# Overflow rounds of a routed mixture of experts: one loop on the chip in place of four unrolled copies

## The chip, the cores and the metric

The kernel runs on one core of a Trainium2 chip. The metric is the device time of one execution in microseconds (us), the median over several runs. Five engines work side by side, each with its own stream of instructions: TensorE (PE for matmuls, PEld for its weight loads), VectorE (DVE), ScalarE (ACT), GpSimd (POOL) and SyncE (SP), which here issues nearly all transfers. They are kept in step by semaphores.

## The reference

Two decoder layers over 512 tokens of width 1024, in float32. A layer has a combined input projection, three kinds of attention, an output projection with a layer norm, and then a mixture of 16 experts of which each token uses two:

```python
gates = jnp.sum(jax.nn.one_hot(expert_idx, N_EXPERTS, dtype=jnp.float32) * w[..., None], axis=1)
h = jax.nn.silu(jnp.einsum('nd,edf->enf', xt, w_gate)) * jnp.einsum('nd,edf->enf', xt, w_up)
h = h * gates.T.astype(h.dtype)[:, :, None]
y = jnp.einsum('enf,efd->nd', h, w_down)
```

Each expert has two 1024 x 256 matrices (gate and up) and one 256 x 1024 matrix (down). How many tokens an expert gets depends on the data.

## The kernel before

A small planner (the class `Flow`) runs while the program is built: every piece of work is a stream of steps with an assumed engine and cost, and the planner writes the instructions of all streams into one fixed order for each engine. Nothing of that order is decided on the chip.

The experts are computed sparsely. Each expert has `CAP` = 96 slots, so the 16 experts fill 1536 rows, which are `NP` = 12 passes of 128 rows. For a pass, GpSimd gathers 128 token rows (`gather`, line 1293), TensorE transposes them (line 1503), multiplies with gate and up (`s_passes`, line 1594), ScalarE and VectorE form silu(gate) times up (lines 1472 and 1473), TensorE transposes that (line 1500) and multiplies with down (`second`, line 1568), and GpSimd scatters the rows to a scratch tensor in HBM (`scatter`, line 1298). SP streams the expert weights ahead of use (lines 1355, 1357 and 1361, `s_load_experts`), as buffers come free. On TensorE the work of one pass stands in the order: transposes of line 1500 and 1503, the down product of the pass before it (line 1568, 32 matmul records), the gate and up product of the next (line 1594, 64 records).

An expert that gets more than 96 tokens is finished by `overflow` (lines 1369 to 1417). It first reads on every engine the largest count of tokens of any expert into a register (line 1370) and branches on it:

```python
many = nc.values_load(mosti[0:1, 0:1], min_val=0, max_val=S)
...
with tc.If(many > CAP):
```

Inside stand ceil((512 - 96) / 128) = 4 rounds. Each round marks which token sits in which of the next 128 overflow slots of every expert (`slot_hot`, line 1385), builds a table of rows by matmuls (`table_mm`), and then runs a loop on the chip over the 16 experts that gathers, multiplies and scatters 128 rows each. The rounds were written out four times by a Python loop; only the loop over experts is a loop on the chip (`tc.For_i`). When no expert has more than 96 tokens, every engine jumps over all of this. Behind the jump stands a short piece that waits for the semaphores that the skipped part would have moved and moves them on; SP's and GpSimd's part of it waits for transfers.

The planner places `overflow` as one step of 0.5 us on TensorE, in the midst of the passes. In the built order it falls, in both layers, between the two halves of a down product of line 1568, ahead of the gate and up product of pass 10 (counted from 0). The planner does not see how many instructions the step holds.

Of the kernel before, what the change touches and what calls it, by code (L numbers as in the profile page):

```python
# [11 lines left out]
OP = mybir.AluOpType  # L12
# [4 lines left out]
P = 128  # L17
D = 1024
S = 512
NT = S // P  # L20
# [4 lines left out]
CAP = 96  # L25
# [170 lines left out]
def body(tc, sb, pp, dr, x, w_in, attn_sinks, c_q_norm_g, c_kv_norm_g, w_uq, w_ukv, w_out, ln1_g, ln1_b,  # L196
         w_router, router_bias, w_gate, w_up, w_down, ln2_g, ln2_b, rope, out):
    nc = tc.nc
    V, A, G, T, SY = nc.vector, nc.scalar, nc.gpsimd, nc.tensor, nc.sync
# [25 lines left out]
    def fixed(*shape):  # L225
        n = 1
        for d in shape:
            n *= d
        return view(take_f(n), *shape)
# [18 lines left out]
    smalls = {}  # L248
# [45 lines left out]
    iotf = fixed(P)  # L294
# [49 lines left out]
    slot_hot = [sb.tile([P, P], BF16, name=f"sl{i}") for i in range(8)]  # L344
    slot_val = [sb.tile([P, 16 * NE], BF16, name=f"rv{i}") for i in range(2)]

    def val(q, w):
        return slot_val[q][:, :16 * w].rearrange("p (k m i e) -> p k m i e", k=4, m=2, i=2)
# [59 lines left out]
    def rshape(w, *shape):  # L408
        n = 1
        for d in shape:  # L410
            n *= d
        v = w[:, :n]
        if len(shape) == 2:
            v = v.rearrange("p (a b) -> p a b", b=shape[1])
        if len(shape) == 3:
            v = v.rearrange("p (a b c) -> p a b c", b=shape[1], c=shape[2])
        return v
# [61 lines left out]
    def layer(l, xready, prev_free):  # L479
# [738 lines left out]
        def table_mm(pt, w):  # L1218
            for j in range(8):
                for m in range(2):  # L1220
                    T.matmul(pt[:, :2 * w], slot_hot[j], val(j // 4, w)[:, j % 4, m].rearrange("p a b -> p (a b)"), start=j + m == 0,
                             stop=j == 7 and m == 1)

        def table_set(pt, ti, w):
            V.tensor_scalar(ti[:, :, :w], pt[:, :2 * w].rearrange("p (a b) -> p a b", b=w), FAR, None, op0=OP.add)
# [66 lines left out]
        def gather(g, idx):  # L1292
            G.indirect_dma_start(out=g, out_offset=None, in_=XD[l][:, :],
                                 in_offset=bass.IndirectOffsetOnAxis(ap=idx, axis=0),
                                 bounds_check=S - 1, oob_is_err=False)

        def scatter(yo, idx):
            return G.indirect_dma_start(out=YD[l][:, :], out_offset=bass.IndirectOffsetOnAxis(ap=idx, axis=0),
                                        in_=yo, in_offset=None, bounds_check=2 * S - 1, oob_is_err=False)
# [69 lines left out]
        def overflow():  # L1369
            many = nc.values_load(mosti[0:1, 0:1], min_val=0, max_val=S)  # L1370
            ps, acc = [g[1] for g in ov["PS"]], [g[1] for g in ov["ACC"]]
            r0, w8, r2 = ov["RAW"][0][1], ov["RAW"][1][1].rearrange("p (a b) -> p a b", b=512), ov["RAW"][2][1]
            w2 = ov["RAW"][1][1].rearrange("p (a b) -> p a b", b=D)
            g, yo, gt = r0[:, :D], r0[:, D:], rshape(r2, KD, P)
            si, hx, ht = r2[:, D:D + FE], r2[:, D + FE:D + 2 * FE], rshape(r2[:, D + 2 * FE:], 2, P)
            with tc.If(many > CAP):  # L1376
                for q in range(NT // 2):

                    V.tensor_tensor(smalls["row", q], smalls["posk", q], smalls["eb", q], op=OP.subtract)
                    oh4 = smalls["oh", q].rearrange("p (k o e) -> p k o e", k=4, o=1).to_broadcast([P, 4, 2, NE])  # L1380
                    V.tensor_scalar(val(q, NE)[:, :, 0], oh4, pcol, None, op0=OP.mult)
                    V.tensor_tensor(val(q, NE)[:, :, 1], oh4, rowc[q].to_broadcast([P, 4, 2, NE]), op=OP.mult)
                for r in range(-(-(S - CAP) // P)):
                    for j in range(8):
                        V.tensor_scalar(slot_hot[j], iotf, float(r * P), smalls["row", j // 4][:, j % 4:j % 4 + 1],
                                        op0=OP.add, op1=OP.is_equal)
                    table_mm(ps[0], NE)
                    table_set(ps[0], tidx[1], NE)
                    with tc.For_i(0, NE, 1) as e:
                        V.tensor_copy(idx2[:, 0:1], tidx[1][:, 0, bass.ds(e, 1)])  # L1390
                        V.tensor_copy(idx2[:, 1:2], tidx[1][:, 1, bass.ds(e, 1)])
                        G.memset(g, 0.0)
                        gather(g, idx2[:, 0:1])
                        for b in range(2):
                            pb = ps[b].rearrange("p (a b) -> p a b", b=P)
                            for j in range(4):
                                T.transpose(pb[:, j], g[:, (4 * b + j) * P:(4 * b + j + 1) * P], ident)
                            A.copy(gt[:, 4 * b:4 * b + 4], pb)
                        for u in range(2):
                            us = slice(u * 512, (u + 1) * 512)  # L1400
                            SY.dma_start(w8[:, :, :FE], w_gate[l, bass.ds(e, 1), us, :].rearrange("o (k p) c -> p (o k) c", p=P))
                            SY.dma_start(w8[:, :, FE:], w_up[l, bass.ds(e, 1), us, :].rearrange("o (k p) c -> p (o k) c", p=P))
                            for j in range(4):
                                k = 4 * u + j
                                T.matmul(acc[0], gt[:, k], w8[:, j], start=k == 0, stop=k == KD - 1)
                        A.activation(si, acc[0][:, :FE], AF.Silu)
                        V.tensor_tensor(hx, si, acc[0][:, FE:], op=OP.mult)
                        pb = ps[0].rearrange("p (a b) -> p a b", b=P)
                        for j in range(2):
                            T.transpose(pb[:, j], hx[:, j * P:(j + 1) * P], ident)  # L1410
                        A.copy(ht, pb[:, :2])
                        SY.dma_start(w2, w_down[l, bass.ds(e, 1)].rearrange("o (k p) c -> p (o k) c", p=P))
                        for n in range(2):
                            for j in range(2):
                                T.matmul(acc[1], ht[:, j], w2[:, j, n * 512:(n + 1) * 512], start=j == 0, stop=j == 1)
                            A.copy(yo[:, n * 512:(n + 1) * 512], acc[1])
                        scatter(yo, idx2[:, 1:2])
# [4 lines left out]
        def s_overflow():  # L1422
            yield E("most")
            yield E("near")
            yield E("gu", NP - 3)
            ov["RAW"] = yield Take(RAW2, 3)
            ov["PS"], ov["ACC"] = [], []
            for _ in range(2):
                ov["PS"].append((yield Take(PS)))
            for _ in range(2):  # L1430
                ov["ACC"].append((yield Take(ACC)))
            e = yield pe(0.5, overflow, [max(flow.free.values())])
            for k in ("A", "V", "G", "D", "GD"):
                flow.free[k] = max(flow.free.get(k, 0.0), e)
            for g in ov["RAW"]:
                put_raw(g, e)
            for g in ov["PS"]:
                PS.put(g, e)
            for g in ov["ACC"]:
                ACC.put(g, e)  # L1440
            flow.set(E("over"), e)
# [335 lines left out]
```

## Time and profile before

| what | value |
|---|---|
| runs: median of 3 (lowest to highest) | 863.41 us (861.07 to 863.6) |
| profiled execution, its own time | 862.1 us |
| its span, first to last instruction | 860.3 us |
| TensorE busy | 821.7 us, 96% of the span |
| mean granted TensorE clock | 0.988 of full |
| expert stage of layer 0 / of layer 1 | about 240 to 412 us / 680 to 828 us of the span |

The profile is of one execution. Busy times are sums over an engine's instructions; TensorE's matmuls are pipelined, so a busy TensorE is not one at its peak. The name PEq (or PEldq, DVEq, ACTq, SPq, POOLq) stands for an engine's sequencer, which does branches, register loads and semaphores; these don't count as busy. q8 and q14 are the queues over which instructions themselves are fetched.

### The profile page before, as it was taken

What the parts mean: (1) busy time and instruction counts of PE and PEld (TensorE: products, weight loads), DVE (VectorE), ACT (ScalarE), POOL (GpSimd) and SP (SyncE); (2) the same over time, 40 slices, a digit from 0 to 9 for tenths busy, and PEclk for the clock granted to TensorE, in tenths of its full rate; (3) what the DMA queues carried; (4) which work ended last, traced back from release to release, by engine and by line L of the source; (5) the groups of instructions that cost most, each with busy time, mean ns of one, the idle gap of its engine ahead of it and who ended that gap; (6) DMA issues with size and microseconds to landing.
All of it is one profiled execution on the core that took longest, in us unless ns stands there. A gap on an engine that the chain in (4) does not pass through costs nothing. (4 is left out here: it accounts for less than half of the span.)

```text
span 860.3 us, 16084 instructions
## 1 busy us (share of the span) xinstructions
PE 821.7 (96%) x6288; PEld 536.8 (62%) x6288; DVE 509.6 (59%) x1504; ACT 315.3 (37%) x790; POOL 103.8 (12%) x135
## 2 busy tenths in 40 slices
PE   7999999999999999979999999999999999999795
PEld 7878886668894333323587889766788743334232
DVE  6799999955681120002998999999458413100057
ACT  4434647963111222212145274677521012221111
POOL 1010102000111111100211001300100111110004
PEclk9999999999999999989999999999999999999898
DMA  8422430175377999976544217010946489999562
GB/s 267 142 77 86 137 134 26 28 266 181 121 252 242 350 370 376 371 266 246 182 102 141 74 50 269 2 50 29 339 147 219 146 306 371 372 372 369 192 265 98
DMA packets 119148, 172.82 MB, mean 201 GB/s; under 512 B 12102, under 2 KB 95558, under 8 KB 119057
## 3 DMA queue, kind: packets, MB, share of 16 engines
q1 hardware_dynamic: 112720, 156.12, 52.8%
q0 software_dynamic: 6336, 15.52, 5.0%
q8 instruction: 53, 0.87, 0.4%
q14 instruction: 39, 0.31, 0.1%
HBM read 154.01 MB, written 25.17 MB: 208 GB/s over the span
## 5 line engine op out<-in xcount | busy, mean ns | idle before, releaser
L283 PE MATMUL bank<-ring,ra 128*128 128x512 f32 (+4 forms) x448 | 167.1, 373 | 0.5 <-ACT fa L605 0.5
L1594 PE MATMUL bank<-fa,ra 128*32 128x512 f32 x1080 | 161.3, 599 | 1.2 <-DVE ra L280 0.7
L284 PE MATMUL bank<-ring,xl 128*128 128x512 f32 (+4 forms) x448 | 157.6, 352 | 0.9 <-DVE xl L452 0.9
L285 PE MATMUL bank<-ring,ra 128*128 128x512 f32 (+4 forms) x448 | 157.9, 353 | 0.0
L279 ACT ACTIVATE fa<-bank 128x512 f32<-128x512 f32 (+3 forms) x170 | 85.4, 516 | 155.9 <-PE bank L441 82.7
L1473 DVE TENSOR_TENSOR fa<-fa,bank 128x256 f32<-128x256 f32 x24 | 10.1, 419 | 214.6 <-ACT fa L1472 214.6
L1594 PEld LDWEIGHTS bank<-fa,ra 128*32 128x32 f32 x1080 | 50.3, 111 | 75.0 <-issue 67.6
L1568 PE MATMUL bank<-fa 128*32 128x512 f32 x504 | 83.8, 625 | 11.1 <-PEq L1376 10.0
L283 PEld LDWEIGHTS bank<-ring,ra 128*128 128x128 f32 x448 | 85.0, 190 | 14.9 <-issue 7.1
L285 PEld LDWEIGHTS bank<-ring,ra 128*128 128x128 f32 x448 | 84.8, 189 | 8.2
L284 PEld LDWEIGHTS bank<-ring,xl 128*128 128x128 f32 x448 | 85.2, 190 | 7.4 <-DVE xl L452 1.3
L441 PE MATMUL bank<-fa 128*128 128x128 f32 (+1 forms) x456 | 71.6, 281 | 7.3 <-DMA fa<-in_x_dram 5.5
L441 PEld LDWEIGHTS bank<-fa 128*128 128x128 f32 (+1 forms) x456 | 55.3, 144 | 24.1 <-issue 6.0
L474 ACT ACTIVATE ring<-fa 128x1024 fp32r<-128x1024 f32 (+4 forms) x56 | 49.4, 897 | 55.7 <-PE bank L284 52.4
L1594 PE MATMUL bank<-ring,ra 128*32 128x512 f32 x360 | 67.1, 592 | 0.0
L1472 ACT ACTIVATE fa<-bank 128x256 f32<-128x256 f32 x24 | 9.2, 384 | 153.0 <-PE bank L1594 153.0
L475 DVE TENSOR_TENSOR ring<-fa,ring 128x1024 fp32r<-128x1024 f32 (+4 forms) x56 | 57.9, 1041 | 7.5 <-ACT ring L474 7.4
L747 DVE MATCH_REPLACE8 aux<-fa,aux 128x256 f32<-128x256 f32 (+2 forms) x96 | 51.6, 540 | 0.0
L746 DVE MAX8 fa<-aux 128x8 f32<-128x256 f32 (+2 forms) x96 | 50.3, 547 | 0.1
L1568 PEld LDWEIGHTS bank<-fa 128*32 128x32 f32 x504 | 19.6, 112 | 46.7 <-issue 44.9
L787 PE MATMUL bank<-fa 64*128 64x256 f32 (+7 forms) x256 | 47.4, 413 | 0.0
L800 ACT ACTIVATE fa<-fa 128x256 f32<-128x256 f32 (+3 forms) x89 | 44.5, 503 | 0.0
(222 smaller groups left out, 1219.3 us busy)
## 6 DMA issues: line engine op xcount, KB each, us to landing
fa<-in_w_gate_dram SPq DMA_DIRECT2D x45, 512.0 KB, 9.4
fa<-in_w_up_dram SPq DMA_DIRECT2D x45, 512.0 KB, 10.4
fa<-in_w_down_dram SPq DMA_DIRECT2D x21, 1024.0 KB, 9.7
xl<-in_w_down_dram SPq DMA_DIRECT2D x9, 1024.0 KB, 11.6
fa<-in_w_out_dram SPq DMA_DIRECT2D x8, 1024.0 KB, 5.9
yd<-fa SPq DMA_DIRECT2D x16, 512.0 KB, 8.3
ring<-in_w_gate_dram SPq DMA_DIRECT2D x15, 512.0 KB, 9.0
ring<-in_w_up_dram SPq DMA_DIRECT2D x15, 512.0 KB, 8.9
```

Source lines behind the costliest of these rows:

```text
L279: return Step([("A", 0.05 + n / 1200, lambda: A.activation(dst, src, AF.Copy)), ("V", 0.12 + n / 960, lambda: V.tensor_copy(dst, src))], a ...
L283: T.matmul(ps, xh, wh, start=start, stop=False)
L284: T.matmul(ps, xl, wh, start=False, stop=False)
L285: T.matmul(ps, xh, wl, start=False, stop=stop)
L441: T.transpose(ps[:n, j, :], s, ident)
L474: yield Step([("A", 0.09 + n / 1200, lambda: A.activation(hv, raw, AF.Copy))], None)
L475: t = yield ve(n, lambda: V.tensor_tensor(lv, raw, hv.bitcast(F32), op=OP.subtract))
L746: yield ve(nk, lambda: V.max(m8, sc))
L747: yield ve(nk, lambda: V.match_replace(sc, m8, sc, MARK))
L787: T.matmul(got[1][:, a * nk:(a + 1) * nk], qs[h], ks[h], start=True, stop=True)
L1568: T.matmul(a[1][cs], ht[:, j, cs], E("raw", e, 2).got[1][:, j, n * 512:(n + 1) * 512], start=j == 0, stop=j == 1)
L1594: T.matmul(acc[1][cs], gh[:, 4 * u + j, cs], E("raw", e, u).got[1][:, j], start=u + j == 0, stop=u + j == 4)
```

## The change

The four rounds become a loop on the chip with the loop over experts inside it. Since the round's number is then no constant, the comparison no longer adds 128 r to the slot number; instead each round subtracts 128 from the token's row (`smalls["row", q]`) after it was compared.

```diff
-                for r in range(-(-(S - CAP) // P)):
+                with tc.For_i(0, -(-(S - CAP) // P), 1):
                     for j in range(8):
-                        V.tensor_scalar(slot_hot[j], iotf, float(r * P), smalls["row", j // 4][:, j % 4:j % 4 + 1],
-                                        op0=OP.add, op1=OP.is_equal)
+                        V.tensor_scalar(slot_hot[j], iotf, smalls["row", j // 4][:, j % 4:j % 4 + 1], None, op0=OP.is_equal)
+
+                    for q in range(NT // 2):
+                        V.tensor_scalar(smalls["row", q], smalls["row", q], float(-P), None, op0=OP.add)
                     table_mm(ps[0], NE)
                     table_set(ps[0], tidx[1], NE)
                     with tc.For_i(0, NE, 1) as e:
```

Outside `overflow` every engine has the same work in the same order; line numbers behind line 1386 grow by two.

TensorE, layer 0, at the jump of line 1376. The rows are instructions in the engine's order (bank is a bank of PSUM; fa, ring, ra and xl are regions of SBUF); before, the end of the fourth copy, the end of the conditional part, and the first work behind it:

```order
L1397 MATMUL bank_73<-fa,ring_1_1932 128x128 x4
L1405 MATMUL bank_71<-ring_3_2103,ring_3_2120 128x512 x8
L1410 MATMUL bank_68<-fa,ring_3_2120 128x128 x2
L1415 MATMUL bank_69<-ring_3_2103,ring_3_2120 128x512 x4
L1389 REGISTER_ALU
L1389 COMPARE_AND_BRANCH
L1389 UNCONDITIONAL_BRANCH
L1376 UNCONDITIONAL_BRANCH
L1568 MATMUL bank_70<-fa 32x512 x8
L1594 MATMUL bank_71<-fa,ra_2148 32x512 x32
```

Now, the end of the one copy that is left:

```order
L1407 MATMUL bank_71<-ring_3_2103,ring_3_2120 128x512 x8
L1412 MATMUL bank_68<-fa,ring_3_2120 128x128 x2
L1417 MATMUL bank_69<-ring_3_2103,ring_3_2120 128x512 x4
L1391 REGISTER_ALU
L1391 COMPARE_AND_BRANCH
L1391 UNCONDITIONAL_BRANCH
L1383 REGISTER_ALU
L1383 COMPARE_AND_BRANCH
L1383 UNCONDITIONAL_BRANCH
L1376 UNCONDITIONAL_BRANCH
L1570 MATMUL bank_70<-fa 32x512 x8
L1596 MATMUL bank_71<-fa,ra_2148 32x512 x32
```

The work behind the jump is the same (1570 and 1596 are the old 1568 and 1594); in front of it three copies of the rounds are gone. In the compiled program, whose instructions are 64 bytes each, the distance from the branch of line 1376 to the place it jumps to is in either layer:

| engine | before | after |
|---|---|---|
| TensorE | 516 instructions, 33.0 KB | 154, 9.9 KB |
| VectorE | 167, 10.7 KB | 74, 4.7 KB |
| ScalarE | 130 (layer 1: 129), 8.3 KB | 59 (58), 3.8 KB |
| GpSimd | 158, 10.1 KB | 71, 4.5 KB |
| SP | 233, 14.9 KB | 99, 6.3 KB |

SP, layer 0, just behind the jump, with the semaphores that it waits for there in brackets (DMAHW0 to DMAHW7 count the landings of transfers that SP issues in turn). Before:

```order
L1376 UNCONDITIONAL_BRANCH [waits DMAHW0_49,DMAHW1_49,DMAHW2_49,DMAHW3_49,DMAHW4_49,DMAHW5_49,DMAHW6_49,DMAHW7_49]
L1355 DMA fa<-in_w_gate_dram 128x4x256 [waits DMAHW7_49,PE_49]
L1357 DMA fa<-in_w_up_dram 128x4x256 [waits DMAHW0_49]
L1361 DMA fa<-in_w_down_dram 128x2x1024 [waits DMAHW1_49]
L521 DMA fa<-in_w_in_dram 128x4x324 [waits DMAHW5_49,DMAHW6_49,DMAHW2_49,PE_49]
```

Now:

```order
L1376 UNCONDITIONAL_BRANCH [waits DMAHW0_49,DMAHW1_49,DMAHW2_49,DMAHW3_49,DMAHW7_49]
L1355 DMA fa<-in_w_gate_dram 128x4x256 [waits DMAHW7_49,PE_49]
L1357 DMA fa<-in_w_up_dram 128x4x256 [waits DMAHW0_49]
L1361 DMA fa<-in_w_down_dram 128x2x1024 [waits DMAHW1_49]
L521 DMA fa<-in_w_in_dram 128x4x324 [waits DMAHW5_49,DMAHW6_49,DMAHW2_49,PE_49]
```

Three semaphores fewer stand there (DMAHW4, 5 and 6, those of the three transfers issued last; in layer 1 it is DMAHW5, 6 and 7). The three transfers behind it, the last weights of expert 15, are the same.

## Rows read from the trace of the kernel before

**Rows 1.** The page's first part: engine, busy us (share), instructions.

```profile
PE 821.7 (96%) x6288; PEld 536.8 (62%) x6288; DVE 509.6 (59%) x1504; ACT 315.3 (37%) x790; POOL 103.8 (12%) x135
```

**Rows 2.** TensorE's waits, expert stages: who, releaser, us, times, longest.

```profile
PE bank L1568 <- PEq L1376: 5.2, 1, 5.2
...
PE bank L1568 <- PEq L1376: 4.8, 1, 4.8
```

**Rows 3.** TensorE in order of time, layers 0 and 1: start, us, instructions, idle.

```profile
360.50 3.64 PE L1568 MATMUL bank<-fa 128*32 128x512 f32 x32
...
370.96 0.44 PE L1500 MATMUL bank<-fa 128*128 128x128 f32 x2
...
372.20 1.93 PE L1568 MATMUL bank<-fa 128*32 128x512 f32 x16
379.30 3.64 PE L1568 MATMUL bank<-fa 128*32 128x512 f32 x16 [5.17 <-PEq L1376]
...
390.78 0.44 PE L1500 MATMUL bank<-fa 128*128 128x128 f32 x2
...
781.65 3.64 PE L1568 MATMUL bank<-fa 128*32 128x512 f32 x32
...
792.26 0.44 PE L1500 MATMUL bank<-fa 128*128 128x128 f32 x2
...
793.50 1.93 PE L1568 MATMUL bank<-fa 128*32 128x512 f32 x16
800.23 3.64 PE L1568 MATMUL bank<-fa 128*32 128x512 f32 x16 [4.80 <-PEq L1376]
...
811.17 0.44 PE L1500 MATMUL bank<-fa 128*128 128x128 f32 x2
```

**Rows 4.** Single microseconds: us, PE, PEld, DVE, ACT, POOL, granted clock, DMA share.

```profile
384.00:385.00 1.00, 1.00 (x8) 0.23 (x4) 0.00 (x0) 0.00 (x0) 0.84 (x1) 0.57 0.33 51
...
804.00:805.00 1.00, 1.00 (x8) 0.23 (x4) 0.00 (x0) 0.53 (x1) 0.20 (x1) 0.65 0.02 7
```

**Rows 5.** Line 1376: engine, operation, ns min/median/max, first and last start.

```profile
L1376 DVEq COMPARE_BRANCH  x2: 63/68/72, 372.5 to 793.6; - x2
L1376 PEldq COMPARE_BRANCH  x2: 6119/6218/6317, 372.8 to 793.9; - x2
...
L1376 SPq COMPARE_BRANCH  x2: 45/49/53, 373.0 to 795.0; - x2
L1376 DVEq EVENT_SEMAPHORE  x2: 21/21/21, 373.1 to 794.1; - x2
...
L1376 SPq EVENT_SEMAPHORE  x8: 17/17/17, 379.6 to 382.6; - x8
...
L1376 SPq EVENT_SEMAPHORE  x8: 17/17/17, 800.7 to 804.8; - x8
```

**Rows 6.** Instruction fetch queues: whole span, then 367:368, 376:379, 791:792.

```profile
q8 instruction: 53, 0.87, 0.4%
q14 instruction: 39, 0.31, 0.1%
...
q8 instruction: 1, 0.02, 7.2%
...
q8 instruction: 1, 0.02, 2.4%
...
q8 instruction: 1, 0.02, 6.0%
```

**Rows 7.** Line 1357 in 783:784 and 787:788: weight transfers, issue and landing.

```profile
L1357 SPq DMA_DIRECT2D fa<-in_w_up_dram x1: 1377/1377/1377, 783.3 to 783.3; - x1
...
DMA to landing us min/median/max: 11.7/11.7/11.7
...
L1357 SPq DMA_DIRECT2D fa<-in_w_up_dram x1: 2734/2734/2734, 787.3 to 787.3; - x1
...
DMA to landing us min/median/max: 10.7/10.7/10.7
```

## The prediction

> **What bounds the kernel now.** The page's first part comes first: TensorE is busy for 821.7 us, 96% of the span, and VectorE, next, for 59% [rows 1]. So a microsecond that TensorE stands still is a microsecond of the kernel, unless something else is late there too. Next come TensorE's waits in the two expert stages. The longest in each is the same: the down product of line 1568 waited 5.2 us in layer 0 and 4.8 us in layer 1 for PEq at line 1376, which is TensorE's own sequencer at the branch [rows 2]. Everything else that it waited for there was well under 1 us at a time. The third view is line 1376 by itself: the branch took TensorE 6317 and 6119 ns, VectorE 72 and 63 ns [rows 5]. The branch was taken on all engines (the overflow part does not run: behind the branch TensorE goes on with line 1568 [rows 3]), so what is waited for is not the count but the place that is jumped to. TensorE had 1.3 us of matmuls queued when the branch began (372.8 against the end of the first half at 372.20 + 1.93 = 374.13); then it stood still.
>
> The fourth view is TensorE in order of time, for the whole price. From a pass's start of line 1568 to its next line 1500 it takes 370.96 - 360.50 = 10.46 us in layer 0 and 792.26 - 781.65 = 10.61 us in layer 1. The pass with the branch takes 390.78 - 372.20 = 18.58 and 811.17 - 793.50 = 17.67 us [rows 3]. The excess is **8.12 us and 7.06 us, 15.18 us together**. [...]
>
> **Why the branch is slow on TensorE alone.** Two engines show a slow jump, and they are the two with the longest jumps in units of their fetches. Instructions come in packets: 0.87 MB in 53 on q8 is 16.4 KB each, 0.31 MB in 39 on q14 about 8 KB [rows 6]. A packet of q8 falls between 376 and 379 us, inside TensorE's stall [rows 6], so q8 is TensorE's and q14 serves the other four. TensorE jumps over 33.0 KB, two of its packets or a little more. SP jumps over 14.9 KB, 1.8 of its packets, and its first semaphore step comes at 379.6 and 800.7, 6.6 and 5.7 us after branches at 373.0 and 795.0 [rows 5]. VectorE jumps over 10.7 KB, 1.3 of its packets, which always ends on another packet than the branch, and its semaphore step comes 0.6 and 0.5 us after the branch [rows 5]. So a jump into the next packet does not wait, one past it does: the next packet seems to be on hand already.
>
> **The change, part by part.** (1) TensorE's jump falls to 154 instructions, 9.9 KB, 0.6 of its packet: it ends on the branch's own packet or the next, as VectorE's does now. Cost by that row: 0.5 to 0.6 us, under the 1.3 us (layer 1: 1.5 us, 795.43 against 793.9) of matmuls that are queued; without that cover it would cost 0.6 us a layer. Upper bound: the 6.3 us of today. I take the near row, nothing on the path. The gap goes, and the low clock that follows it: 15.2 us gained.
>
> (2) The packet behind the target is asked for later relative to its use. In layer 0 the last packet before the branch came at 367 us [rows 6]; if a packet follows its request by the 4 us that it does at the branch (372.8 to 376 or later), the branch is 8 to 10 us, or at some 20 instructions per us (212 loads and matmuls in 10.46 us) 160 to 200 instructions, into a packet of 256. The target, 154 on, then lies 60 to 100 into the next, and the 160 or so left last 8 us against a fetch of 6.3 us. In layer 1 it came at 791 us, so the branch was 5 to 7 us or 100 to 140 instructions in; 362 instructions fewer in layer 0 put it at the very start or end of a packet. If at the start, 70 to 100 are left behind the target, 3.5 to 5 us plus 1.5 us queued, and the fetch may come up to 1.3 us late. I take nothing for it and keep 0 to 1.3 us.
>
> (3) SP's jump falls to 99 instructions, 0.8 of its packet, so its 6.6 and 5.7 us go too, and it waits behind it for five landings in place of eight. Its next transfers, three of expert 15, wait for the down product in any case, which ends 7 us earlier; they move with TensorE and stay hidden.
>
> (4) Weights must not become the new wait. The tightest is layer 1, pass 10: expert 14's up halves land at 783.3 + 11.7 = 795.0 and 787.3 + 10.7 = 798.0 [rows 7]. Without the gap line 1568 is through at 793.50 + 3.64 = 797.1 [rows 3], when line 1594 needs the first; the second is needed half of line 1594 later, some 3.4 us (half of 10.46 - 3.64), at 800.5. Both are in time, by 2.1 and 2.5 us. Price: nothing.
>
> (5) Added work (subtracting 128 from the rows, the second loop's control) stands inside the part that is jumped over: nothing.
>
> The sum, against the profiled execution: 862.1 - 15.2 = 846.9 us. The median of the runs shown is 863.41, 1.3 above that execution, so the forecast is 848.2, **848 us**.
>
> [...]
>
> **The rivals.** *The wait belongs to the jump itself on TensorE, whatever its length* (a taken branch empties what is held and the target is fetched anew). For it: no short jump of TensorE is in the trace, and its packets differ from VectorE's. Against it: VectorE's jump also leaves its packet and does not wait, and SP's waits as TensorE's does, so length sorts the four engines' cases that the rows show. Time: 863 us, within 0.3%. Chance 0.06.
>
> *One layer keeps the stall*, since the packets' borders lie differently in the two layers and the target falls on the next packet in one and on the same in the other. Time: 863.4 - 7.1 or - 8.1, about 856 us. Chance 0.05.
>
> *The weights take over.* TensorE arrives 5 us earlier at expert 14 and 15 than the transfers were ever tested for. If landings slip by 4 to 5 us beside the transfers that SP now issues earlier, TensorE waits 2 to 3 us a layer and the clock may fall again. Time: 852 to 856 us. Against it: those transfers are issued after expert 14's. Chance 0.04.
>
> *Slower:* the target is still fetched, and the fetch comes behind more transfers. SP, no longer held, issues 1.5 MB and more at once; transfers of that stage land 10.7 and 11.7 us after issue [rows 7], against 6.3 us for the fetch. Each stall would grow by up to 4 us. It decides only if the target is not on hand and SP's transfers get ahead of the packet. Time: 866 to 871 us. Chance 0.03.
>
> **How the numbers follow.** The forecast keeps 0.82. Its own range is 846 us (the lowest run, 861.07, less 15.2) to 850 (the late packet of 1.3 us and the spread of the runs). The range of 8 in 10 takes in weights late on top: 845.5 to 853. A measurement of this kernel tells about 0.3%, 2.6 us, from no change, as its three runs spread over 2.5 us. Faster by more: 0.82 + 0.05 + 0.04 = 0.91; the same 0.06; slower 0.03.
>
> **What would show it.** Right: TensorE's branch of line 1376 takes under 0.1 us in both layers, its wait for PEq is gone, the granted clock stays at full from 372 to 385 and 780 to 800 us, and the pass with the branch takes 10.5 us. SP's first step behind its branch comes within 1 us, or waits for a landing. Wrong: a branch of 6 us again (first rival), in one layer only (second), TensorE's waits naming a transfer at line 1594 (third), or a longer one (fourth).

## The result

The changed kernel takes 847.77 us (median of 4 runs, 847.3 to 848.98) against 863.5 us for the kernel before on the same chip: a ratio of 0.9822, 95% interval 0.9802 to 0.9841, or 15.7 us less. The forecast was 848 us. The profiled execution took 847.3 us, 14.8 us less than the one of before.

The head of the page of the changed kernel and its row of TensorE's granted clock in 40 slices, with the same row of the kernel before as the last line:

```profile
span 845.5 us, 16062 instructions
PE 817.0 (97%) x6288; PEld 534.9 (63%) x6288; DVE 510.3 (60%) x1504; ACT 315.4 (37%) x790; POOL 103.6 (12%) x135
...
PEclk9999999999999999999999999999999999999998
...
PEclk9999999999999999989999999999999999999898
```

The number of matmul records is the one of before [rows 1]: no work has gone. TensorE's busy time is 4.7 us less, since the granted clock shows no low slice until the last one.

Line 1376 in the changed kernel (engine, operation, count, ns min/median/max, first and last start), to set beside [rows 5]:

```profile
L1376 SPq EVENT_SEMAPHORE  x10: 17/17/17, 373.6 to 789.8; - x10
...
L1376 DVEq COMPARE_BRANCH  x2: 63/68/72, 372.4 to 785.6; - x2
L1376 PEldq COMPARE_BRANCH  x2: 342/348/353, 372.7 to 786.0; - x2
...
L1376 DVEq EVENT_SEMAPHORE  x2: 21/21/21, 373.0 to 786.2; - x2
L1376 SPq COMPARE_BRANCH  x2: 45/49/53, 373.1 to 786.9; - x2
L1376 PEldq EVENT_SEMAPHORE  x2: 51/51/51, 374.1 to 787.5; - x2
```

TensorE's branch took 6317 and 6119 ns and takes 353 and 342. From the branch's start to the semaphore step behind it there are 1.4 us (372.7 to 374.1) and 1.5 us (786.0 to 787.5), more than VectorE's 0.6 us. That is not the jump's own time: the matmuls that were queued end at 372.12 + 1.93 = 374.05 and 785.54 + 1.93 = 787.47 (rows below), and the step comes within 0.1 us of that end. SP's first step came 0.5 us after its branch in either layer.

TensorE in order of time in the two passes with the branch, changed kernel, to set beside [rows 3] (1570, 1596 and 1502 are the old 1568, 1594 and 1500):

```profile
372.12 1.93 PE L1570 MATMUL bank<-fa 128*32 128x512 f32 x16
374.22 1.93 PE L1570 MATMUL bank<-fa 128*32 128x512 f32 x16 [0.18 <-PEq L1376]
375.94 7.10 PE L1596 MATMUL bank<-fa,ra 128*32 128x512 f32 x64
382.97 0.44 PE L1502 MATMUL bank<-fa 128*128 128x128 f32 x2
...
785.54 1.93 PE L1570 MATMUL bank<-fa 128*32 128x512 f32 x16
787.65 1.93 PE L1570 MATMUL bank<-fa 128*32 128x512 f32 x16 [0.18 <-PEq L1376]
789.37 7.10 PE L1596 MATMUL bank<-fa,ra 128*32 128x512 f32 x64
796.39 0.44 PE L1502 MATMUL bank<-fa 128*128 128x128 f32 x2
```

The gaps of 5.17 and 4.80 us are 0.18 us each. The second half takes 1.93 us as the first does, where it took 3.64 us [rows 3] at a granted clock of 0.50 (the rows on the price, below). From line 1570 to line 1502 it is 10.85 us in both layers, against 18.58 and 17.67 us [rows 3]: 7.73 + 6.82 = 14.55 of the 14.8 us by which the span is shorter.

Two stretches of the changed kernel around the branches (us, PE, PEld, DVE, ACT, POOL, granted clock, DMA share, GB/s):

```profile
372.00:376.00 4.00, 3.82 (x38) 1.13 (x40) 0.54 (x1) 1.20 (x2) 0.00 (x0) 1.00 1.06 384
785.00:789.00 4.00, 3.82 (x38) 1.35 (x40) 0.91 (x2) 1.42 (x3) 0.00 (x0) 1.00 1.05 368
```

The clock stays at full, and the transfer engines are as full as they were (1.06 in 372 to 376 us before). The instruction fetch queues over the whole span:

```profile
q8 instruction: 51, 0.84, 0.4%
q14 instruction: 31, 0.25, 0.1%
```

TensorE fetched two packets fewer and the other four engines together eight [rows 6].

### The profile page after: what moved, and what is told of

Read it like the earlier page. It is cut to its first block, busy times and chain, and to the rows that moved or that the text cites. A ratio compares the mean times of both kernels' runs of the same rounds, so it can differ in the third digit from the quotient of the medians.

```text
span 845.5 us, 16062 instructions
## 1 busy us (share of the span) xinstructions
PE 817.0 (97%) x6288; PEld 534.9 (63%) x6288; DVE 510.3 (60%) x1504; ACT 315.4 (37%) x790; POOL 103.6 (12%) x135
## 5 line engine op out<-in xcount | busy, mean ns | idle before, releaser
L1475 DVE TENSOR_TENSOR fa<-fa,bank 128x256 f32<-128x256 f32 x24 | 10.1, 420 | 200.3 <-ACT fa L1474 200.3
L283 PEld LDWEIGHTS bank<-ring,ra 128*128 128x128 f32 x448 | 85.0, 190 | 14.8 <-issue 7.1
L1570 PE MATMUL bank<-fa 128*32 128x512 f32 x504 | 80.4, 595 | 1.5 <-DVE fa L280 0.6
```

Of the source, the lines that this page charges most:

```text
L283: T.matmul(ps, xh, wh, start=start, stop=False)
L1570: T.matmul(a[1][cs], ht[:, j, cs], E("raw", e, 2).got[1][:, j, n * 512:(n + 1) * 512], start=j == 0, stop=j == 1)
```

## The experiments

All were run beside the kernel before, in the same way; ratios are to it, with 95% intervals.

**The loop, with TensorE's jump made long again.** If the distance is what counts, the loop must lose its gain when instructions that never run are put between the branch and its target on TensorE alone.

```diff
                     table_mm(ps[0], NE)
+                    for _ in range(181):
+                        T.matmul(ps[1][:, :P], ones, ones, start=True, stop=True)
                     table_set(ps[0], tidx[1], NE)
```

> The changed kernel, with 181 small matmuls more in the part that is jumped over, so that TensorE's jump is 516 instructions (33.0 KB) as before; the other four engines keep their short jumps. None of the added matmuls runs. If the length of TensorE's jump decides: 862 to 864 us, TensorE's branch of line 1376 takes 6.1 to 6.3 us in both layers and the clock falls behind it, while SP's first step comes within 1 us of its branch. If the four copies' many branches and semaphores, or SP's and GpSimd's waits, made the time: 847 to 849 us. If SP's stall of 6 us had a share: between 850 and 862 us.

Measured: 862.84 us, ratio 0.9993 (0.9983 to 1.0003). The whole gain is gone. Its line 1376:

```profile
L1376 SPq EVENT_SEMAPHORE  x10: 17/17/17, 373.6 to 799.3; - x10
...
L1376 PEldq COMPARE_BRANCH  x2: 6252/6304/6357, 372.4 to 795.5; - x2
...
L1376 SPq COMPARE_BRANCH  x2: 45/49/53, 373.1 to 796.4; - x2
L1376 PEldq EVENT_SEMAPHORE  x2: 51/51/51, 378.8 to 801.8; - x2
```

TensorE's branch is back at 6.3 us, while SP goes on 0.5 us after its own. So neither the loop nor the fewer branches and semaphores, nor SP's shorter wait, made the time: the length of TensorE's jump did.

The instruction fetch queues of this run:

```profile
q8 instruction: 53, 0.87, 0.4%
q14 instruction: 31, 0.25, 0.1%
```

Against the changed kernel only TensorE's instructions are more, and only q8 has more packets. That q8 is TensorE's queue was argued in the prediction from one packet; here it is shown.

**No branch at all.** The register load, the branch and the overflow part are left out (`overflow` returns at once). This leaves out the rounds for experts with more than 96 tokens, which do not run with this data.

> The kernel before without register load, branch and overflow part (the rounds for experts with more than 96 tokens are left out; with this data they do not run). If after the change nothing is left of the branch but 0.18 us of waiting a layer: 847 to 847.8 us, 0 to 0.5 us under the changed kernel. If the conditional part has other costs (register loads, semaphore steps behind it, TensorE's 1.4 us between branch and next step): 2 us or more under it, 845 us or less.

Measured: 847.01 us, ratio 0.9818 (0.9802 to 0.9834). The changed kernel's 0.9822 lies within that. What the conditional part still costs is under what can be measured, as two gaps of 0.18 us are. Without the branch the down product of layer 0 runs through (line 1521 is the old 1568):

```profile
371.46 3.64 PE L1521 MATMUL bank<-fa 128*32 128x512 f32 x32
```

**Three copies.** `range(3)` in place of the four rounds; the fourth round is left out, and does not run.

> Three copies in place of four (the fourth round is left out; it does not run). TensorE's jump is 387 instructions, 24.8 KB, 1.5 packets. If the place decides that is jumped to, with packet borders as the prediction counted them: the branch stands some 165 (layer 0) and 243 (layer 1) instructions into a packet of 256, 387 on lies in the packet after the next in both, so both layers stall as before: 862 to 864 us. If the cost goes with the number of copies: a quarter of 15.7 us less, 859 to 860 us. If every jump of more than one packet stalls: 862 to 864 us too.

Measured: 862.09 us, ratio 0.9985 (0.9972 to 0.9999). Line 1376:

```profile
L1376 PEldq COMPARE_BRANCH  x2: 6243/6645/7047, 372.0 to 793.5; - x2
```

Both layers stall in full, with a quarter of the copies gone: the cost does not go with their number.

**Two copies.** `range(2)`; the last two rounds are left out, and do not run.

> Two copies in place of four (the last two rounds are left out; they do not run). TensorE's jump is 258 instructions, 16.5 KB, just over one packet. If packet borders decide, the branch stands some 147 and 96 instructions into its packets and 258 on lies in the next one in both layers: 847 to 849 us. If a jump of more than one packet stalls: 862 to 864 us. If cost goes with copies: 855 to 856 us.

Measured: 847.34 us, ratio 0.9807 (0.9775 to 0.9839). Line 1376:

```profile
L1376 PEldq COMPARE_BRANCH  x2: 352/812/1272, 372.5 to 785.4; - x2
...
L1376 PEldq EVENT_SEMAPHORE  x2: 51/51/51, 373.9 to 787.0; - x2
```

The whole gain with half of the copies still there: with these packet borders it is a step between 258 and 387 instructions, not a slope, and it lies above the length of one packet (16.5 KB are jumped over without a stall, and the packets of q8 are 16.4 KB [rows 6]). One of the two branches took 1.27 us, which the queued matmuls covered: the gap behind it is 0.18 us too.

**Loop in layer 0, three copies in layer 1.** Is it the length, or the packet in which the target lies?

```diff
+                if l == 0:
+                    with tc.For_i(0, -(-(S - CAP) // P), 1):
...
+                else:
+                    for r in range(3):
...
```

> Layer 0 as changed (jump of 154 instructions), layer 1 with three copies (387 instructions, 24.8 KB, as in the run with three copies in both layers). With 233 instructions fewer ahead of it than there, the branch of layer 1 stands some 10 instructions into a packet, and 387 on lies in the next one. If the packet borders decide: no stall in either layer, 847 to 849 us. If the length alone decides (over one packet stalls): layer 1 stalls, 854 to 856 us. If cost goes with copies: 859 us less 7.8, about 853 us.

Measured: 854.85 us, ratio 0.9906 (0.9882 to 0.9931). Layer 1 stalled:

```profile
L1376 PEldq COMPARE_BRANCH  x2: 352/3280/6207, 372.6 to 786.6; - x2
...
L1376 PEldq EVENT_SEMAPHORE  x2: 51/51/51, 374.0 to 792.8; - x2
```

That is against what packet borders were to give, unless the place of the border was wrong. The prediction had put layer 1's branch of the changed kernel at "the very start or end of a packet"; I had taken the start for this run. The end fits as well, and the next run decides.

**The same with the border moved.** 24 matmuls that never run in layer 0's part move layer 1's branch on by 48 instructions; layer 1 itself is unchanged.

```diff
                         table_mm(ps[0], NE)
+                        for _ in range(24):
+                            T.matmul(ps[1][:, :P], ones, ones, start=True, stop=True)
                         table_set(ps[0], tidx[1], NE)
```

> The run with the loop in layer 0 and three copies in layer 1 once more, with 24 small matmuls (48 instructions) more in the part that layer 0 jumps over (202 instructions in place of 154); none of them runs. Layer 1 is as there: a jump of 387 instructions, 24.8 KB. The runs so far say that the branch of layer 1 stood at the end of a packet there (some 248 instructions in, not 10), so 387 on lay in the packet after the next. Moved on by 48 it stands some 40 into the next packet, and 387 on lies in the packet behind that. If packet borders decide: no stall in either layer, 847 to 849 us. If a jump of more than one packet stalls wherever it starts: layer 1 stalls again, 854 to 856 us.

Measured: 850.05 us, ratio 0.9836 (0.9803 to 0.9869). Its line 1376:

```profile
L1376 PEldq COMPARE_BRANCH  x2: 352/382/412, 372.9 to 787.3; - x2
...
L1376 PEldq EVENT_SEMAPHORE  x2: 51/51/51, 374.3 to 788.9; - x2
```

TensorE's longest waits in 660 to 830 us (who, releaser, us, times, longest; 1635 and 1609 are the old 1594 and 1568):

```profile
PE bank L1635 <- DMA fa<-in_w_up_dram: 1.2, 1, 1.2
PE bank L1635 <- issue: 0.7, 1, 0.7
```

TensorE's instruction fetches in 790 to 792 us:

```profile
q8 instruction: 1, 0.02, 4.0%
```

The same jump of 387 instructions no longer stalls (412 ns at most, against 6207 ns), and all that differs is 48 instructions elsewhere. So the length alone does not decide. No trace shows a border itself; as the borders are counted here, the packet that the target lies in decides. The time is some 2 us above the changed kernel's, though the changed kernel's ratio lies within the interval. Two things in this trace are near that size: a wait of 1.2 us for weights, which ends at 778.7 us, ahead of the branch, and 0.7 us in which TensorE waited for nothing that the profile shows, at 793 us. The packet of instructions began at 791.0 us and took 1.3 us; TensorE went on at 793.7 us, 1.4 us after its end. At a stalled branch it went on 1.4 to 1.6 us after (see the branch at a place with few transfers, below), so I take the second for the late packet of the prediction's point (2). It also comes where the border should be by estimate: the trace has 70 instructions of TensorE between the step behind the jump and the gap, and a branch some 40 into its packet of 256 with a jump of 387 leaves some 85 up to the border. The wait for weights was not followed further.

**SP's long jump alone.** Small transfers that never run make SP's jump 236 instructions and its wait eight landings, as before.

```diff
                         SY.dma_start(w2, w_down[l, bass.ds(e, 1)].rearrange("o (k p) c -> p (o k) c", p=P))
+                        for _ in range(116):
+                            SY.dma_start(w8[:, 0, :FE], w_gate[l, 0, :P, :])
```

> The changed kernel, with small transfers added to the part that is jumped over, so that SP's jump is 236 instructions (233 before) and SP waits for all eight landings behind it, as before; TensorE's jump stays at 154. None of the transfers runs. If SP's stall is hidden: SP's first step comes 5 to 7 us after its branch again, its last three weight transfers go out some 6 us later than in the changed kernel, and the time stays at 847 to 849 us. If the earlier transfers are needed: TensorE waits for them at line 1596 and the time is 850 us or more.

Measured: 847.67 us, ratio 0.9813 (0.9781 to 0.9846). SP at line 1376:

```profile
L1376 SPq EVENT_SEMAPHORE  x16: 17/17/17, 379.2 to 795.2; - x16
...
L1376 SPq COMPARE_BRANCH  x2: 45/49/53, 373.6 to 786.3; - x2
```

SP's transfers of layer 0 behind the branch (start, us):

```profile
381.96 0.39 SPq L1355 DMA_DIRECT2D fa<-in_w_gate_dram  x1
382.41 0.49 SPq L1357 DMA_DIRECT2D fa<-in_w_up_dram  x1
382.94 0.50 SPq L1361 DMA_DIRECT2D fa<-in_w_down_dram  x1
```

SP's first step comes 5.6 us after its branch again (8.4 us in layer 1, more than was expected), and the last three weight transfers go out at 382 us; in the changed kernel the first of them goes out at 376.2 us:

```profile
376.20 0.38 SPq L1355 DMA_DIRECT2D fa<-in_w_gate_dram  x1
```

Nothing waits for them. SP's stall was there, but hidden; all of the gain is TensorE's. How much of SP's stall is the jump and how much the landings that its steps wait for is not shown: with two copies SP's first step came 0.5 us after its branch in layer 0 and 7.7 us after it in layer 1.

One more row of this run bears on the short jump, which is the changed kernel's own on TensorE:

```profile
L1376 PEldq COMPARE_BRANCH  x2: 345/874/1402, 372.7 to 785.4; - x2
```

In layer 0 it took 1.40 us, and the gap was 0.26 us. A packet of instructions had begun at 371.6 us, 1.1 us before the branch, and ended at 372.6 us; the branch ended 1.4 us after that. In the changed kernel's layer 0, where the branch took 0.35 us, the packet before it had begun at 367.1 us. So a short jump waited here too, with a packet that had ended 0.1 us before it; that the one comes from the other is not shown.

**The branch at a place with few transfers.** Four copies, but the conditional part behind the last gate and up product (`E("gu", NP - 1)` in place of `NP - 3` in `s_overflow`).

> Four copies as before, with the whole conditional part moved to behind the last gate and up product of each layer, when nearly all weights have landed and few transfers run. TensorE's jump is 516 instructions and its target lies past the next packet in both layers. If most of the 6.2 us is the packet's way through busy transfer queues: TensorE's branch takes 3 to 4 us there, with a gap of 1.5 to 3 us in each layer, and the time is 855 to 859 us, unless the scattered rows are read back later too. If the fetch has a fixed time: 6 us again and 862 to 864 us.

Measured: 861.16 us, ratio 0.9968 (0.9951 to 0.9985). Line 1376:

```profile
L1376 PEldq COMPARE_BRANCH  x2: 3339/3599/3859, 392.6 to 811.7; - x2
```

TensorE in order of time behind the branch of layer 0, and at a later gap of layer 1:

```profile
396.61 0.62 PE L1568 MATMUL bank<-xl,fa 128*32 128x512 f32 x2 [1.58 <-PEq L1376]
...
821.02 0.62 PE L1568 MATMUL bank<-xl,fa 128*32 128x512 f32 x2 [3.56 <-issue]
```

The stretches of the two branches, with granted clock, DMA share and GB/s as the last columns:

```profile
392.00:396.00 4.00, 3.03 (x30) 0.74 (x22) 0.79 (x4) 0.46 (x2) 0.00 (x0) 1.00 0.48 160
811.00:815.00 4.00, 3.44 (x34) 0.90 (x23) 0.40 (x2) 0.38 (x1) 0.00 (x0) 1.00 0.21 62
```

TensorE's instruction fetches in 812 to 813 and 818 to 819 us, and before in 376 to 377 us (share of 16 engines; 7.2% of a microsecond are 1.15 us of one):

```profile
q8 instruction: 1, 0.02, 5.9%
...
q8 instruction: 1, 0.02, 6.6%
...
q8 instruction: 1, 0.02, 7.2%
```

The branch took 3.3 and 3.9 us here, as was expected if most of the 6.2 us was the packet's way through busy queues (the DMA share is 0.48 and 0.21 in these stretches, against 1.06 around layer 0's branch before); the time of 861.16 us was not as expected (855 to 859 us). The packets themselves show what a stall is made of. Amid the weights the packet began 3.8 and 3.6 us after the branch (376.6 and 797.5 us); here, with the transfer engines half busy or less, 1.5 and 1.0 us after it (394.05 and 812.75 us). Once begun it took 0.9 to 1.2 us in all four cases, and TensorE's step came 1.4 to 1.6 us after its end. Amid the weights the branch took 2.5 and 2.8 us longer, and 2.3 and 2.6 us of that were the wait until the packet began.

The gap at the branch of layer 0 is 1.58 us, and the clock stays up. In layer 1 a second gap of 3.56 us follows. A packet began at 818.6 us and took 1.1 us, and the gap ends 1.3 us after that. With the border where the two runs with 387 instructions place it, the branch stands by estimate some 222 instructions into a packet there and the target, 516 on, some 30 short of a border; the trace has 25 instructions between the step behind the jump and the gap, so I take it for a late packet again. Behind this gap the granted clock is 0.50, up to 825 us:

```profile
824.00:825.00 1.00, 1.00 (x4) 0.00 (x0) 0.00 (x0) 0.00 (x0) 0.00 (x0) 0.50 1.07 426
```

The time barely fell. In the run that follows the place itself is tried.

**The loop at the late place.** The changed kernel, moved in the same way.

> The changed kernel (one loop, jump of 154 instructions) with the conditional part at the late place of the run with four copies behind the last gate and up product. There 6.9 us were gained in layer 0 and lost again elsewhere. If the late place itself costs (SP's and GpSimd's work queued behind the branch): 853 us or more, though no branch stalls. If the four copies' jump cost it there as well, by short stalls, late packets and the clock: 847 to 849 us.

Measured: 850.29 us, ratio 0.984 (0.98 to 0.988), between the two expectations; the changed kernel's ratio lies within its interval. So the late place costs some 2 us by itself, with an interval of 3.5 us to either side, and the four copies cost some 11 us there too (861.16 against 850.29 us). TensorE at line 1376, and the matmuls that were queued there:

```profile
L1376 PEldq COMPARE_BRANCH  x2: 236/288/339, 393.9 to 808.9; - x2
L1376 PEldq EVENT_SEMAPHORE  x2: 51/51/51, 396.4 to 811.7; - x2
...
395.95 0.44 PE L1502 MATMUL bank<-fa 128*128 128x128 f32 x2
...
811.20 0.44 PE L1502 MATMUL bank<-fa 128*128 128x128 f32 x2
```

The branch took 0.24 and 0.34 us, and the step came 2.5 and 2.8 us after its start, again at the end of the queued matmuls (396.39 and 811.64 us). The two traces of the late place, set side by side, also show where the 11 us went. The gap of 1.58 us in layer 0 is no loss: with the loop TensorE waits 1.07 us at the same place for ScalarE. Behind it the run with four copies falls back 9.9 us on TensorE. 3.7 us are the second gap of layer 1, and 2.1 us the granted clock of 0.50 behind it. Of the others, 1.7 us come at line 284 between the layers, where TensorE waits 2.3 us for VectorE in place of 0.5, 1.0 us at a wait for gathered rows and 0.9 us at one for weights; why these are longer was not followed.

## Why the prediction was right, point by point

**The bound and the price.** 15.18 us were read from two passes; the passes gave back 14.55 us, the span 14.8 us, the medians 15.7 us with an interval of 1.7 us to either side. Reading the excess of the whole pass, not the gap alone, was the step that mattered: the gaps are 5.17 + 4.80 = 9.97 us [rows 3], and the other 5.2 us, a third of the price, was the clock behind them: it was at 0.50 of full and rose again within the two microseconds of [rows 4]. The kernel before, behind either gap (us, PE, PEld, DVE, ACT, POOL, granted clock, DMA share, GB/s):

```profile
380.00:381.00 1.00, 1.00 (x9) 0.24 (x5) 0.00 (x0) 0.00 (x0) 0.00 (x0) 0.50 0.29 92
...
801.00:802.00 1.00, 1.00 (x12) 0.31 (x8) 0.00 (x0) 0.00 (x0) 0.00 (x0) 0.50 0.26 87
```

The clock followed the gap: it fell to 0.50 in or behind gaps of 5.17, 4.80 and 3.56 us (the last with the late branch), and stayed at full behind gaps of 1.58, 0.7 and 0.18 us.

**(1) TensorE's jump.** Right in kind: no packet of q8 runs between the branch and TensorE's next work; the next ones begin at 376.6 and 789.8 us, where TensorE had gone on at 374.22 and 787.65 us. "Under 0.1 us" for the branch itself was wrong, it took 0.34 and 0.35 us. The size of 0.5 to 0.6 us, taken from VectorE's step behind its branch, can't be set against TensorE's 1.4 to 1.5 us: in the changed kernel, with two copies, with SP's long jump and with the late loop alike, TensorE's step comes within 0.15 us of the end of the queued matmuls, however long that is. The cover of 1.3 us therefore hid the jump, and what came through is 0.18 us a layer behind the end of the queue, 0.4 us in all. That the cover was enough is in part luck: in the run with SP's long jump the same branch took 1.40 us in one layer.

**(2) The next packet.** Taken as nothing, and nothing in the changed kernel shows it. In other runs it seems to cost: those with the border moved and with the late branch have gaps of 0.7 and 3.6 us, which end 1.4 and 1.3 us after a packet's end; at the stalled branches it was 1.4 to 1.6 us. The border in layer 1 was rightly called uncertain; the start, which was priced, was the wrong one of the two. The count behind it, made from times, was somewhat high: from the runs I estimate layer 0's branch at some 147 instructions into its packet, and the prediction had 160 to 200.

**(3) and (4) SP and the weights.** Right: SP's stall went and was worth nothing, as its own run shows, though the prediction's reading of it as a slow jump alone is not shown. Right too: no weight was late in the changed kernel. With the border moved and with the late branch TensorE waited 1.2 and 1.1 us for weights of an earlier pass of layer 1, so weights came close to the time of use there. **(5)** Right: the run without the branch is not measurably faster.

**The rivals.** A wait that belongs to the jump itself falls with the changed kernel and with two copies. One layer alone stalling did not happen here, but was made to happen (854.85 us, where the prediction had about 856). Late weights and a longer fetch did not come.

In all of these runs TensorE's jumps sort by packets as the borders are counted here. A jump of 516 instructions stalled each time (6.1 to 6.4 us amid the weights, 3.3 and 3.9 us at the late place); one of 387 stalled three times (6.2 to 7.0 us) and once did not (0.41 us); one of 258 stalled in neither layer (0.35 and 1.27 us). These runs decide nothing on SP's packets: over a jump of 14.9 KB its first step came 6.6 and 5.7 us after its branch [rows 5], but SP also waits for landings there.

## What to carry to other kernels

Code that is jumped over was not free here: on TensorE, which bounds this kernel, two jumps of 516 instructions cost 15.7 us, and jumps of 154 and 258 cost waits of 0.18 to 0.26 us each. So look at the branches of the engine that bounds a kernel, and try to keep rarely run ones short there; a loop is one way to do it. Read the price from the whole stage: behind gaps of 3.56 to 5.17 us on TensorE the granted clock was 0.50. When such a gap appears or goes after an edit elsewhere, count where the packet borders have moved before looking at the edit: a jump of 387 took 6.2 or 0.4 us with 48 instructions' difference elsewhere.

## What had not been expected

In the seven waits of TensorE whose packets are given above, it went on only 1.3 to 1.6 us after the packet's end, more than the 0.9 to 1.3 us that the packet itself took. And 48 instructions that never run, in another layer, decided whether a branch cost 6.2 us or 0.4 us.
